# Matrix LSTM layer: head norm on ScalarE behind the next inner products, output gate and skip multiplied out where the gates are made

## The chip, the cores and the metric

The kernel runs on one core of a Trainium2 chip, in one launch. The metric is the device time of an execution in microseconds (us); several executions are timed and the median is given. One further execution is recorded by the hardware profiler, and all rows of a profile come from that one. Engines are named as in the profile: PE is TensorE (matrix products), PEld its loading of weights, DVE VectorE, ACT ScalarE, POOL GpSimd, SP SyncE, which here only issues transfers (DMA).

## The reference

A decoder trunk of two layers, 1024 tokens, width 1024, float32. Each layer has a mixer, a cross-attention into 256 memory tokens and a squared-ReLU MLP; each of these is `h = h + RMSNorm_post(f(RMSNorm_pre(h)))`. The change is in the mixer of the second layer, a matrix LSTM with 4 heads of 256:

```python
def _odd_mixer(hn, w_in, conv_w, conv_b, w_q, w_k, w_v, w_gates, b_gates, g_hnorm, skip, w_out):
    x_m, z = jnp.split(hn @ w_in, 2, axis=-1)
    x_c = jax.nn.silu(_causal_conv(x_m, conv_w, conv_b))
    q, k = per-head products of x_c with w_q, w_k;  v = per-head product of x_m with w_v
    gates = jnp.concatenate([q, k, v], axis=-1).reshape(B, S, 3 * MIX_WIDTH) @ w_gates + b_gates
    h = _mlstm_cell(q, k, v, i_pre, f_pre)
    h = _layernorm(h, g_hnorm.reshape(H, DH)).reshape(B, S, MIX_WIDTH)
    out = (h + skip * x_c) * jax.nn.silu(z)
    return out @ w_out
```

(The lines on q, k and v are shortened.) `_mlstm_cell` runs over chunks of tokens. In each it forms the decayed inner products of queries and keys (`w_intra`), `num = w_intra @ v + w_inter * (q @ C)`, a denominator, `h = num / max(|den|, exp(-m))`, and then carries the state `C` of 256 x 256 a head to the next chunk. `_layernorm` takes the mean and variance of a token over the 256 features of a head.

## The kernel before, in words

Every float32 matrix product that needs its precision is done as three products of rounded parts: a tile is split into a high part (ACT copies it, rounded, line 137) and a low part (DVE or POOL subtracts the two, line 143), and `acc3` (lines 149 to 151) issues high x high, high x low and low x high. So ACT and DVE, and POOL for some weights, have a piece of work for each tile that PE is to use.

SBUF is shared out as 34 units of about 4 KB a partition (`self.u`), 12 weight tiles (`self.wt`) and 3 raw tiles. Weights come through `Stream`: a load on SP's queue into a raw tile, then a split; `Stream.next()` keeps a fixed number of tiles ahead. All engines work in order on lists that the tile scheduler makes from the program text: it runs a model of the engines and takes the ready instruction that stands first in the text, so instructions move ahead of others where their inputs are ready, and the text's order is a priority and not the order itself.

`mix1` has these parts:

- **Projections and gates.** For each head, `front` makes x_m and x_c (convolution, SiLU), feature-major, half of the tokens (512) at a time; `ready` splits them and stores x_c to DRAM (`xd`); `back` makes the gate pre-activations, q and v and stores them. Between `ready` and `back` stands one half of `gate(j)`: 24 products for 128 features of z, SiLU by ACT and DVE (lines 396 to 400), and a store of silu(z) into `zd`. `gate(0)` to `gate(3)` are done in the four heads' turns, `gate(4)` to `gate(7)` behind them, between the first loads of the chunk sweep.
- **Chunk sweep**, 8 chunks of 128 tokens, 8 PSUM banks. `load(c)` brings q, k, v and the decay row; `decay(c)` makes the exponentials; `within(c)` makes the inner products S of queries and keys, multiplies them with the decay (line 1665) and splits them, and makes the weighted keys; `across(c)` multiplies with v and the carried state into `nm` (ACT copies the state's part from PSUM, line 1730, DVE adds the other from PSUM, line 1734), updates C (line 1743) and splits it. The head norm stands at the end of `across`: statistics (lines 1751 to 1758), the power -1/2 on POOL (`rstd`, lines 187 and 188), and four `tensor_scalar` on DVE, one a head (line 1762). `turn(c)` transposes `nm` on PE and multiplies it with the norm's gain out of PSUM (line 1775). `self.side(1, ...)` puts in a piece of independent work for the cross-attention (kt, vt, wk, vo; its weights' low parts are made on POOL, line 143, in pairs of 128x1024).
- **End and output projection.** `skips(c)` loads x_c and silu(z) of a chunk (xg, zg), and POOL makes skip * x_c * silu(z) in two products (lines 1704 and 1705). `gated(c)` multiplies hT with zg, adds xg (DVE, lines 1711 and 1712) and splits the sum into m. `out_proj` multiplies with w_out1 (lines 372 to 375), two PSUM tiles of two banks; `tail` makes the post-norm, adds the residual on POOL (line 306) and prepares the next sub-layer.

The sweep's order in the text:

```python
for c in range(NT):
    across(c)
    if c < NT - 2:
        load(c + 2)
    self.side(1, SIDE_LSTM[c])
    if c < NT - 1:
        within(c + 1)
    if c < NT - 2:
        decay(c + 2)
    if c:
        turn(c - 1)
    ...
```

Of the kernel before, what the change touches and what calls it, by code (L numbers as in the profile page):

```python
# [7 lines left out]
F32 = mybir.dt.float32  # L8
# [3 lines left out]
AF = mybir.ActivationFunctionType  # L12
ALU = mybir.AluOpType
AX = mybir.AxisListType

P = 128
D = 1024
S = 1024
NT = S // P
HALF = 512  # L20
# [57 lines left out]
class Trunk:  # L78
# [81 lines left out]
    def stream_of(self, sub):  # L160

        T, l = self.T, int(sub[-1])
        if sub[:2] == "xa":
            return Stream(self, [self.kv[l][0][j // 4, j % 4].rearrange("p a b -> p (a b)") for j in range(8)], 1, "dve", (6, 7))
        if sub[:3] == "ffn":
            first = [(g, p) for ps in (SEVEN[:2], SEVEN[2:]) for g in (0, 1) for p in ps]
            return Stream(self, first + [(g, p) for g in range(2, GROUPS) for p in SEVEN], 3, make=self.up_weights(l))
        if l == 0:
            return Stream(self, [T["w_in0"][j] for j in (4, 5, 6, 7, 0, 1, 2, 3)] + [T["w_gvr"][j] for j in range(8)], 2)
        return Stream(self, [T["w_in1"][j] for j in (0, 1, 2, 3, 8, 4, 5, 9, 6, 7, 10, 11, 12, 13, 14, 15)], 1)  # L170

    def prefetch(self, n, lo_eng=None):

# [1270 lines left out]
    def mix1(self):  # L1444
        nc, T = self.nc, self.T
        mm = nc.tensor.matmul
        cw, cb = self.const("conv_w"), self.const("conv_b")
        gh, skip = self.const("g_hnorm"), self.const("skip")
        bgt = self.const("b_gates")
        tmask = self.const("tmask")  # L1450
        W = self.take("mix1")

        qd, xd, zd = (self.dram(n, [NT, P, 8, P]) for n in ("qd", "xd", "zd"))
        vd = self.dram("vd", [NT, P, 4, 256])

        def put(dst, half, head, t):
# [5 lines left out]
        with self.psum(6, 1):  # L1462
            gacc = self.u([100, S], F32, "gacc")
            heads, gates = {}, {}
# [83 lines left out]

            def gate(j, halves=(0, 1)):

                if not halves[0]:
                    gates[j] = W.next(), self.u([P, 2, HALF], F32, "sz")
                w, sz = gates[j]
                for half in halves:
                    self.silu(sz[:, half, :], self.feature_major(w, half, "z"), self.t2())
                    nc.sync.dma_start(zd[4 * half:4 * half + 4, :, j, :].rearrange("c p t -> p c t"), sz[:, half, :].rearrange("p (c t) -> p c t", t=P))
                if half:
                    del gates[j]

# [5 lines left out]
            for head in range(4):  # L1565
                if 0 < head < 3:
                    front(head + 1, 0)
                    front(head + 1, 1)
                ops = ready(head, 0)
                gate(head, (0,))  # L1570
                back(head, 0, ops, ws)
                ops = ready(head, 1)
                gate(head, (1,))
                if head < 3:
                    nxt = weights(head + 1)
                back(head, 1, ops, ws)
                ws = nxt
                del heads[head]
# [8 lines left out]
            ig, lf, m, b, tmp = row  # L1587
# [16 lines left out]
            x, y = lf, ig  # L1604
# [75 lines left out]
                            nc.vector.scalar_tensor_tensor(kw[1][:, h, :], k, cl[:, 2, h:h + 1], kw[0][:, h, :].bitcast(F32), ALU.mult, ALU.subtract)  # L1680
                ch[c] = (qp, va, cl, wp, kw)

            gate(4)
            self.side(1, 1)
            load(0)
            gate(5)
            decay(0)
            self.side(1, 1)
            gate(6)
            within(0)  # L1690
            gate(7)
        self.hn = [None, None]
# [1 line left out]
        hT = {}  # L1694
        ms = {}

        sk = {}

        def skips(c):

            xg, zg = self.u([P, 8, P], F32, "xg"), self.u([P, 8, P], F32, "zg")
            for t, src in ((xg, xd), (zg, zd)):
                nc.sync.dma_start(t.rearrange("p a b -> p (a b)"), src[c].rearrange("p a b -> p (a b)"))
            nc.gpsimd.tensor_tensor(xg, xg, skip.unsqueeze(2).broadcast_to([P, 8, P]), ALU.mult)
            nc.gpsimd.tensor_tensor(xg, xg, zg, ALU.mult)
            sk[c] = xg, zg

        def gated(c):

            h, (xg, zg) = hT.pop(c), sk.pop(c)  # L1710
            nc.vector.tensor_tensor(h, h, zg, ALU.mult)
            nc.vector.tensor_tensor(h, h, xg, ALU.add)
            ms[c] = self.parts([P, 8, P], "m")
            self.split(*ms[c], h)

        with self.psum(*PS_LSTM):
# [3 lines left out]
            hbs, wo = {}, []  # L1720

            def across(c):

                qp, va, cl, wp, kw = ch.pop(c)
                nm = self.u([P, 4, 258], F32, "nm")
                for h in range(4):
                    ps = self.p1("num")
# [9 lines left out]
                if c < NT - 1:  # L1737
                    for h in range(4):
                        for e in range(2):
                            ps = self.p1("C")  # L1740
                            self.acc3(ps[:, 0:258], [(tuple(x[:, h, e * P:e * P + P] for x in kw), tuple(x[:, h, :] for x in va))])
                            if c:
                                nc.vector.scalar_tensor_tensor(C[h][:, e, :], C[h][:, e, :], be[:, c, h:h + 1], ps[:, 0:258], ALU.mult, ALU.add)
                            else:
                                nc.vector.tensor_copy(C[h][:, e, :], ps[:, 0:258])
                        self.split(Cp[h][:, 0], Cp[h][:, 1], C[h])
                st = self.sm([P, 4, 4], name="stm1")
                bn = self.sm([P, 4, 6], name="bn")

# [8 lines left out]
                nc.vector.tensor_tensor(s, s, w, ALU.mult)  # L1758
                self.rstd(s, s)
                nc.vector.tensor_tensor(s, s, w, ALU.mult)  # L1760
                for h in range(4):
                    nc.vector.tensor_scalar(nm[:, h, 0:256], nm[:, h, 0:256], st[:, h, 0:1], st[:, h, 3:4], ALU.subtract, ALU.mult)
                hbs[c] = nm

            def turn(c):

                nm = hbs.pop(c)
                hT[c] = self.u([P, 8, P], F32, "hT")
                for g in range(2):
                    ps = self.p1("hT").rearrange("p (a b) -> p a b", b=P)  # L1770
                    for a in range(4):
                        k = 4 * g + a
                        nc.tensor.transpose(ps[:, a, :], nm[:, k // 2, k % 2 * P:k % 2 * P + P], self.ident)
                    w = slice(4 * g, 4 * g + 4)
                    nc.vector.tensor_tensor(hT[c][:, w, :], ps, gh[:, w].unsqueeze(2).broadcast_to([P, 4, P]), ALU.mult)

            load(1)
            decay(1)
# [6 lines that stand above are left out]
                    within(c + 1)  # L1785
                if c < NT - 2:
                    decay(c + 2)
                if c:
                    turn(c - 1)
                if c >= NT - 2:  # L1790
                    skips(c - NT + 2)
                if c == NT - 1:
                    gated(0)
                if c == NT - 2:
                    wo += [self.fetch(T["w_out1"][k], "dve", self.u) for k in (0, 1)]
# [145 lines left out]
```

## Time and profile before

| | |
|---|---|
| median of 3 runs | 2979.53 us (2977.46 to 2980.94) |
| the profiled execution | 2979.67 us; span from first to last instruction 2977.9 us |
| mean granted TensorE clock | 0.980 |
| busy over the span | PE 96%, DVE 64%, ACT 47%, POOL 30% |
| projections and gates | about 1557 to 1812 us |
| chunk sweep | about 1812 to 1997 us |
| its end and the output projection | about 1997 to 2112 us |
| transfers | 385.09 MB, mean 129 GB/s |

A row of the timeline gives start, length, engine, line, operation, output and inputs, and in brackets the time that the engine stood still before it and what ended that. A row by tile or line gives the shortest, median and longest duration in ns. A row of waits gives the total in us, how often, and the longest. In the table of stretches each engine's busy time is followed by its number of instructions; the clock is 1.00 at full speed. Since PE is the busiest engine, the idle time of another engine costs nothing by itself.

### The profile page before, as it was taken

How to read it: one execution, taken by the hardware profiler on the slowest of the kernel's cores; microseconds unless marked ns; L12 is line 12 of the kernel's file. 1: busy time of each engine (PE TensorE's matmuls, PEld its weight loads, DVE VectorE, ACT ScalarE, POOL GpSimd, SP SyncE). 2: the span in 40 equal slices, each digit the busy share in tenths (PEclk: the TensorE clock that was granted, in tenths of full speed). 3: DMA queues.
4: the chain of work that ended last, by engine and by line, in shares of the span. 5: the costliest groups of instructions: out<-in, count | busy, mean ns of one | idle time of the engine just before them, and what ended most of it. 6: DMA issues, size and time to landing. Idle time of an engine off the chain costs nothing. (4 is left out here: it accounts for less than half of the span.)

```text
span 2977.9 us, 37928 instructions
## 1 busy us (share of the span) xinstructions
PE 2846.6 (96%) x14470; PEld 2355.4 (79%) x14470; DVE 1909.4 (64%) x2348; ACT 1402.7 (47%) x2391; POOL 898.2 (30%) x674
## 2 busy tenths in 40 slices
PE   7998999999999999999999999889999999999998
PEld 6777888888887888787867888887788788878776
DVE  4237788754347443799876657887733744458995
ACT  4346666633346455433445565543433655544332
POOL 2204545233330000167050113357533100006723
PEclk9998999999999999999999999999999999999999
DMA  4264544352322333531163345547323233263204
GB/s 160 97 165 147 168 141 148 116 197 71 109 104 90 109 113 136 203 114 64 52 223 96 122 144 178 189 163 251 113 63 121 85 108 112 103 231 111 98 17 142
DMA packets 165222, 385.09 MB, mean 129 GB/s; under 512 B 16748, under 2 KB 66316, under 8 KB 165040
## 3 DMA queue, kind: packets, MB, share of 16 engines
q1 hardware_dynamic: 146608, 349.10, 35.0%
q10 hardware_dynamic: 18432, 33.56, 2.9%
q8 instruction: 114, 1.87, 0.3%
q14 instruction: 68, 0.56, 0.1%
HBM read 267.86 MB, written 113.69 MB: 128 GB/s over the span
## 5 line engine op out<-in xcount | busy, mean ns | idle before, releaser
L143 DVE TENSOR_TENSOR wl<-blk,wh 128x1024 fp32r<-128x1024 f32 x276 | 451.7, 1659 | 320.0 <-ACT wh L137 320.0
L493 POOL TENSOR_TENSOR blk<-blk 128x1024 f32<-128x1024 f32 x80 | 252.4, 3183 | 869.0 <-DVE wl L143 863.5
L137 ACT ACTIVATE wh<-blk 128x1024 fp32r<-128x1024 f32 x276 | 281.8, 1054 | 327.6 <-PE op L561 188.7
L560 PE MATMUL up<-hnh,wh 128*128 128x512 f32 x896 | 356.0, 398 | 9.6 <-ACT hnh L137 5.0
L561 PE MATMUL up<-hnl,wh 128*128 128x512 f32 x896 | 354.5, 396 | 4.8 <-DVE hnl L143 4.8
L562 PE MATMUL up<-hnh,wl 128*128 128x512 f32 x896 | 353.4, 395 | 0.0
L561 PE MATMUL op<-wl,wh 128*128 128x512 f32 x784 | 307.9, 393 | 9.7 <-DVE wl L143 9.6
L560 PE MATMUL op<-wh 128*128 128x512 f32 x784 | 306.3, 395 | 6.2 <-ACT wh L137 6.2
L562 PE MATMUL op<-wh,wl 128*128 128x512 f32 x784 | 306.0, 390 | 0.0
L137 ACT ACTIVATE wh<-raw 128x1024 fp32r<-128x1024 f32 (+1 forms) x163 | 170.6, 1058 | 138.1 <-DMA raw<-hd 25.9
L143 POOL TENSOR_TENSOR wl<-raw,wh 128x1024 fp32r<-128x1024 f32 x66 | 158.9, 2420 | 223.6 <-ACT wh L137 208.3
L560 PEld LDWEIGHTS up<-hnh,wh 128*128 128x128 f32 x896 | 169.1, 189 | 51.3 <-ACT hnh L137 11.4
L561 PEld LDWEIGHTS up<-hnl,wh 128*128 128x128 f32 x896 | 169.3, 189 | 45.5 <-DVE hnl L143 6.3
L562 PEld LDWEIGHTS up<-hnh,wl 128*128 128x128 f32 x896 | 169.3, 189 | 40.1
L143 DVE TENSOR_TENSOR wl<-raw,wh 128x1024 fp32r<-128x1024 f32 (+1 forms) x97 | 126.6, 1315 | 99.7 <-ACT wh L137 99.3
L561 PEld LDWEIGHTS op<-wl,wh 128*128 128x128 f32 x784 | 148.0, 189 | 47.1 <-DVE wl L143 16.4
L560 PEld LDWEIGHTS op<-wh 128*128 128x128 f32 x784 | 149.1, 191 | 39.0 <-ACT wh L137 8.2
L562 PEld LDWEIGHTS op<-wh,wl 128*128 128x128 f32 x784 | 147.8, 188 | 30.5
L187 POOL TENSOR_SCALAR st<-st 128x1 f32<-128x1 f32 x99 | 41.6, 421 | 361.6 <-ACT hn L303 307.4
L306 POOL TENSOR_TENSOR h<-h,hn 128x1024 f32<-128x1024 f32 x47 | 128.4, 2732 | 33.5 <-DVE hn L305 26.2
L673 DVE TENSOR_TENSOR acc<-acc,op 128x512 f32<-128x512 f32 x192 | 123.8, 676 | 4.3 <-PE op L562 4.1
L287 DVE SCALAR_TENSOR_TENSOR hn<-h,st,gain 128x1024 f32<-128x1024 f32 x48 | 101.8, 2122 | 26.1 <-POOL st L188 24.8
(440 smaller groups left out, 6993.5 us busy)
## 6 DMA issues: line engine op xcount, KB each, us to landing
blk<-in_ffn_w_dram SPq DMA_DIRECT2D x120, 512.0 KB, 4.3
h<-h SPq DMA_DIRECT2D x80, 512.0 KB, 4.1
hd<-t ACTq DMA_DIRECT2D x128, 256.0 KB, 2.9
blk<-hd SPq DMA_DIRECT2D x56, 512.0 KB, 4.2
raw<-in_w_in_dram SPq DMA_DIRECT2D x24, 512.0 KB, 4.1
h<-in_x_dram SPq DMA_DIRECT2D x16, 512.0 KB, 6.3
raw<-in_xa_w_k_dram SPq DMA_DIRECT2D x16, 512.0 KB, 3.7
raw<-in_xa_w_v_dram SPq DMA_DIRECT2D x16, 512.0 KB, 3.8
```

The costliest lines, as they stand in the source:

```text
L137: nc.scalar.activation(hi, src, AF.Copy)
L143: e.tensor_tensor(lo, src, hi.bitcast(F32), ALU.subtract)
L187: self.nc.gpsimd.tensor_scalar(dst, src, EPS, None, ALU.add)
L287: nc.vector.scalar_tensor_tensor(hn, h, st[:, 1:2], gpre, ALU.mult, ALU.mult)
L306: nc.gpsimd.tensor_tensor(h, h, t, ALU.add)
L493: eng.tensor_tensor(out, a, b, op)
L560: mm(ps, lh, rh, start=start and not i, stop=False, skip_group_check=True)
L561: mm(ps, lh, rl, start=False, stop=False, skip_group_check=True)
L562: mm(ps, ll, rh, start=False, stop=i == n - 1, skip_group_check=True)
L673: nc.vector.tensor_tensor(dst, dst, ps[i], ALU.add)
```

## The change

The head norm leaves `across` and becomes `norm(c)`, called after `decay(c + 2)` and ahead of `turn(c - 1)`. Its last step, (x - mean) * s, is done on ACT as Identity with scale s and bias -mean * s; DVE makes the bias in one new 128x4 product. `gate(j)` now makes two products for each half: silu(z) times the norm's gain (ACT, stored to `zd`), and skip * x_c * silu(z) (DVE, stored to a new `bd`); both stores are issued by ACT instead of one by SP. In the heads' turns `gate` takes j = 0, 2, 4, 6, whose x_c lies in SBUF, and behind them j = 1, 3, 5, 7, whose x_c is loaded back from `xd`; the weight stream is reordered to match. `norm(c)` loads the chunk's `zd` into the tile hT, and `turn` multiplies the transposed tile with it instead of with the gain. `skips(c)` loads one tile, `bd`, and POOL's two products are gone; `gated(c)` only adds.

```diff
@@ -167,7 +167,7 @@
             return Stream(self, first + [(g, p) for g in range(2, GROUPS) for p in SEVEN], 3, make=self.up_weights(l))
         if l == 0:
             return Stream(self, [T["w_in0"][j] for j in (4, 5, 6, 7, 0, 1, 2, 3)] + [T["w_gvr"][j] for j in range(8)], 2)
-        return Stream(self, [T["w_in1"][j] for j in (0, 1, 2, 3, 8, 4, 5, 9, 6, 7, 10, 11, 12, 13, 14, 15)], 1)
+        return Stream(self, [T["w_in1"][j] for j in (0, 1, 2, 3, 8, 4, 5, 10, 6, 7, 12, 14, 9, 11, 13, 15)], 1)
 
     def prefetch(self, n, lo_eng=None):
 
@@ -1450,7 +1450,8 @@
         tmask = self.const("tmask")
         W = self.take("mix1")
 
-        qd, xd, zd = (self.dram(n, [NT, P, 8, P]) for n in ("qd", "xd", "zd"))
+
+        qd, xd, zd, bd = (self.dram(n, [NT, P, 8, P]) for n in ("qd", "xd", "zd", "bd"))
         vd = self.dram("vd", [NT, P, 4, 256])
 
         def put(dst, half, head, t):
@@ -1548,12 +1549,24 @@
 
             def gate(j, halves=(0, 1)):
 
+                def cols(dst, half):
+                    return dst[4 * half:4 * half + 4, :, j, :].rearrange("c p t -> p c t")
+
                 if not halves[0]:
-                    gates[j] = W.next(), self.u([P, 2, HALF], F32, "sz")
-                w, sz = gates[j]
+                    gates[j] = W.next(), self.u([P, 2, HALF], F32, "sz"), self.u([P, 2, HALF], F32, "bz")
+                w, sz, bz = gates[j]
                 for half in halves:
-                    self.silu(sz[:, half, :], self.feature_major(w, half, "z"), self.t2())
-                    nc.sync.dma_start(zd[4 * half:4 * half + 4, :, j, :].rearrange("c p t -> p c t"), sz[:, half, :].rearrange("p (c t) -> p c t", t=P))
+                    if j % 2:
+                        xc = bz[:, half, :]
+                        nc.sync.dma_start(xc.rearrange("p (c t) -> p c t", t=P), cols(xd, half))
+                    else:
+                        xc = heads[j // 2][2][half][:, 0, :]
+                    z, x = sz[:, half, :], bz[:, half, :]
+                    self.silu(z, self.feature_major(w, half, "z"), self.t2())
+                    nc.vector.scalar_tensor_tensor(x, z, skip[:, j:j + 1], xc, ALU.mult, ALU.mult)
+                    nc.scalar.activation(z, z, AF.Copy, scale=gh[:, j:j + 1])
+                    for dst, t in ((zd, z), (bd, x)):
+                        nc.scalar.dma_start(cols(dst, half), t.rearrange("p (c t) -> p c t", t=P))
                 if half:
                     del gates[j]
 
@@ -1567,10 +1580,10 @@
                     front(head + 1, 0)
                     front(head + 1, 1)
                 ops = ready(head, 0)
-                gate(head, (0,))
+                gate(2 * head, (0,))
                 back(head, 0, ops, ws)
                 ops = ready(head, 1)
-                gate(head, (1,))
+                gate(2 * head, (1,))
                 if head < 3:
                     nxt = weights(head + 1)
                 back(head, 1, ops, ws)
@@ -1680,13 +1693,13 @@
                             nc.vector.scalar_tensor_tensor(kw[1][:, h, :], k, cl[:, 2, h:h + 1], kw[0][:, h, :].bitcast(F32), ALU.mult, ALU.subtract)
                 ch[c] = (qp, va, cl, wp, kw)
 
-            gate(4)
+            gate(1)
             self.side(1, 1)
             load(0)
-            gate(5)
+            gate(3)
             decay(0)
             self.side(1, 1)
-            gate(6)
+            gate(5)
             within(0)
             gate(7)
         self.hn = [None, None]
@@ -1698,18 +1711,13 @@
 
         def skips(c):
 
-            xg, zg = self.u([P, 8, P], F32, "xg"), self.u([P, 8, P], F32, "zg")
-            for t, src in ((xg, xd), (zg, zd)):
-                nc.sync.dma_start(t.rearrange("p a b -> p (a b)"), src[c].rearrange("p a b -> p (a b)"))
-            nc.gpsimd.tensor_tensor(xg, xg, skip.unsqueeze(2).broadcast_to([P, 8, P]), ALU.mult)
-            nc.gpsimd.tensor_tensor(xg, xg, zg, ALU.mult)
-            sk[c] = xg, zg
+            sk[c] = self.u([P, 8, P], F32, "bg")
+            nc.sync.dma_start(sk[c].rearrange("p a b -> p (a b)"), bd[c].rearrange("p a b -> p (a b)"))
 
         def gated(c):
 
-            h, (xg, zg) = hT.pop(c), sk.pop(c)
-            nc.vector.tensor_tensor(h, h, zg, ALU.mult)
-            nc.vector.tensor_tensor(h, h, xg, ALU.add)
+            h = hT.pop(c)
+            nc.vector.tensor_tensor(h, h, sk.pop(c), ALU.add)
             ms[c] = self.parts([P, 8, P], "m")
             self.split(*ms[c], h)
 
@@ -1744,6 +1752,11 @@
                             else:
                                 nc.vector.tensor_copy(C[h][:, e, :], ps[:, 0:258])
                         self.split(Cp[h][:, 0], Cp[h][:, 1], C[h])
+                hbs[c] = nm, cl
+
+            def norm(c):
+
+                nm, cl = hbs[c]
                 st = self.sm([P, 4, 4], name="stm1")
                 bn = self.sm([P, 4, 6], name="bn")
 
@@ -1758,21 +1771,24 @@
                 nc.vector.tensor_tensor(s, s, w, ALU.mult)
                 self.rstd(s, s)
                 nc.vector.tensor_tensor(s, s, w, ALU.mult)
+
+                nc.vector.scalar_tensor_tensor(w, st[:, :, 0], -1.0, s, ALU.mult, ALU.mult)
                 for h in range(4):
-                    nc.vector.tensor_scalar(nm[:, h, 0:256], nm[:, h, 0:256], st[:, h, 0:1], st[:, h, 3:4], ALU.subtract, ALU.mult)
+                    nc.scalar.activation(nm[:, h, 0:256], nm[:, h, 0:256], AF.Identity, bias=st[:, h, 2:3], scale=st[:, h, 3:4])
+                hT[c] = self.u([P, 8, P], F32, "hT")
+                nc.sync.dma_start(hT[c].rearrange("p a b -> p (a b)"), zd[c].rearrange("p a b -> p (a b)"))
                 hbs[c] = nm
 
             def turn(c):
 
                 nm = hbs.pop(c)
-                hT[c] = self.u([P, 8, P], F32, "hT")
                 for g in range(2):
                     ps = self.p1("hT").rearrange("p (a b) -> p a b", b=P)
                     for a in range(4):
                         k = 4 * g + a
                         nc.tensor.transpose(ps[:, a, :], nm[:, k // 2, k % 2 * P:k % 2 * P + P], self.ident)
                     w = slice(4 * g, 4 * g + 4)
-                    nc.vector.tensor_tensor(hT[c][:, w, :], ps, gh[:, w].unsqueeze(2).broadcast_to([P, 4, P]), ALU.mult)
+                    nc.vector.tensor_tensor(hT[c][:, w, :], ps, hT[c][:, w, :], ALU.mult)
 
             load(1)
             decay(1)
@@ -1785,6 +1801,7 @@
                     within(c + 1)
                 if c < NT - 2:
                     decay(c + 2)
+                norm(c)
                 if c:
                     turn(c - 1)
                 if c >= NT - 2:
```

## The prediction

> **What bounds the kernel now.** I read the page first (engines' shares), then busy time by stretch over the odd mixer, then PE's waits there, then the timelines of DVE, POOL and PE around one gap. The page says that TensorE (PE) is nearly always busy, so only time in which PE stands still or runs at a lower granted clock can be won.
>
> ```profile
> PE 2846.6 (96%) x14470; PEld 2355.4 (79%) x14470; DVE 1909.4 (64%) x2348; ACT 1402.7 (47%) x2391; POOL 898.2 (30%) x674
> ```
>
> The stretches are: projections and gates (front), the step over to the chunk sweep, the sweep, its end with the loading of w_out1, and the output projection. Columns: length, busy time of PE, PEld, DVE, ACT, POOL, granted clock, DMA.
>
> ```profile
> 1557.00:1812.00 255.00, 249.59 (x1212) 203.84 (x1211) 153.37 (x214) 141.17 (x243) 36.41 (x30) 1.00 0.42 130
> 1812.00:1840.00 28.00, 22.70 (x172) 21.79 (x172) 25.27 (x49) 15.74 (x29) 8.72 (x6) 0.94 0.58 188
> 1840.00:1997.00 157.00, 142.35 (x1059) 137.58 (x1060) 136.40 (x291) 88.93 (x152) 68.31 (x40) 0.95 0.52 176
> 1997.00:2036.00 39.00, 31.13 (x144) 25.20 (x144) 29.11 (x38) 15.14 (x20) 25.92 (x11) 0.87 0.71 252
> 2036.00:2112.00 76.00, 70.05 (x317) 55.84 (x316) 64.36 (x43) 25.01 (x45) 63.30 (x39) 1.00 0.50 178
> ```
>
> PE loses 157 - 142.35 = 14.7 us of standing in the sweep and 0.05 x 157 = 7.9 by its clock; at the sweep's end 7.9 and 0.13 x 39 = 5.1; in the projection 6.0 and nothing. That makes 22.5 + 13.0 + 6.0 = 41.5 us, all there is to win. The front stands only 5.4 us. Who ends PE's waits (total us, times, longest), first in the sweep, then behind it:
>
> ```profile
> PE C L149 <- DVE nm L1734: 14.4, 5, 3.1
> PE num L149 <- DVE vt L143: 2.3, 1, 2.3
> ```
> ```profile
> PE op L375 <- DVE ml L143: 4.6, 4, 2.2
> PE vo L149 <- DVE nm L1734: 4.5, 1, 4.5
> PE op L373 <- DVE wl L143: 3.2, 1, 3.2
> PE tp L219 <- DVE hn L287: 1.3, 1, 1.3
> ```
>
> So five gaps of 2.9 us wait for DVE's add that empties PSUM (L1734). What holds DVE there, with POOL and PE beside it:
>
> ```profile
> 1862.81 5.05 DVE L1762 TENSOR_SCALAR nm<-nm,stm 128x256 f32<-128x256 f32 x4
> 1867.78 0.41 DVE L1734 TENSOR_TENSOR nm<-nm,num 128x258 f32<-128x258 f32 x1
> ```
> ```profile
> 1862.27 2.41 POOL L143 TENSOR_TENSOR wl<-raw,wh 128x1024 fp32r<-128x1024 f32 x1 [2.36 <-PE num L151]
> ...
> 1864.68 2.38 POOL L143 TENSOR_TENSOR wl<-raw,wh 128x1024 fp32r<-128x1024 f32 x1
> ```
> ```profile
> 1868.25 0.58 PE L149 MATMUL C<-vah,kwh 128*128 128x258 f32 x1 [3.13 <-DVE nm L1734]
> ```
>
> Four normalising instructions (L1762), directly ahead of the adds, take 5.05 us while POOL runs two subtractions of 2.4 us. All of L1762 (shortest, median, longest in ns), and then its busy time on DVE in the sweep:
>
> ```profile
> L1762 DVE TENSOR_SCALAR nm<-nm,stm x32: 397/408/2503, 1826.7 to 2014.0; 128x256 f32<-128x256 f32 x32
> ```
> ```profile
> 1840.00:1997.00 157.00, 31.50 (x24) 0.95 0.52 176
> ```
>
> Undisturbed, one takes 0.397 us, so four would take 1.6; the longest waits out a whole POOL operation, and the median 0.408 hides it. In the sweep that comes to 31.5 us for six chunks, 5.25 us each. These, not the adds, make the gap. The Trainium skill (SBUF — State Buffer, "Who interferes with whom") states that a DVE instruction in a 2-port mode, or with two SBUF inputs, and a GpSimd instruction that reads SBUF block each other for a whole instruction, and that ACT never waits so. By that rule the move is worth the blocked time too, and the 5.05 beside 2.41 and 2.38 agrees.
>
> **The change, step by step.**
>
> *Sweep: L1762 to ACT, and the norm moved.* DVE loses 5.25 us a chunk where a gap is 2.9, so 2.35 us are to spare. Against this stand the statistics, which the new order puts behind `within` and `decay`. They exist now, spread between the C updates:
>
> ```profile
> L1755 DVE BATCH_NORM_STATS2 bn<-nm 128x6 f32<-128x256 f32 x32 | 13.0, 415 | 0.1
> L1665 DVE TENSOR_TENSOR ew<-ew,S 128x512 f32<-128x512 f32 x7 | 4.8, 684 | 16.0 <-PE S L1664 16.0
> L1756 DVE BATCH_NORM_AGGREGATE stm<-bn 128x2 f32<-128x6 f32 x32 | 5.2, 168 | 0.0
> L1752 DVE TENSOR_TENSOR stm<-stm,cl 128x4 f32<-128x4 f32 x8 | 2.2, 273 | 0.0
> L1757 DVE TENSOR_TENSOR stm<-stm 128x4 f32<-128x4 f32 x8 | 1.3, 160 | 0.1
> ```
>
> For a chunk that is 4 x (0.415 + 0.168) = 2.3 us and seven small ones (one of them the new product) near 0.16: about 3.5 us. If they lie in DVE's wait for S (16.0 / 7 = 2.3 us a chunk), the gap goes; if all lie ahead of the adds, 3.5 - 2.35 = 1.1 us of each gap stays. The clock loss follows the gaps. I take 70% of 22.5: **-16**, ends 0 and -22.5. Next would be PE itself: DVE keeps (136.4 - 31.5) of 157.
>
> On ACT come four Identity instructions a chunk, SBUF to SBUF, which the trace lacks. Nearest rows: the same width without a scale tile, and with one:
>
> ```profile
> L1736 ACT ACTIVATE nm<-num x4: 364/380/394, 1815.3 to 1816.1; 128x258 f32<-128x258 f32 x4
> L1730 ACT ACTIVATE nm<-num,cl x28: 457/482/532, 1834.1 to 1997.2; 128x258 f32<-128x258 f32 x28
> ```
>
> I take 0.48, the row with a tile as scale, ends 0.36 and 0.53: 1.9 us a chunk in an engine busy 88.9 of 157; hidden. What is queued behind them on ACT is the draining of num (L1730); PE would wait for that if they came late. The Trainium skill (ScalarE: Activation LUTs, "What ACT_TABLE_LOAD costs") gives 186 ns, 0.833 ns an element and 93 ns a pointer operand; an estimate from that page is 0.585 us with two pointers, 2.3 us a chunk, and the sum would be the same.
>
> SP gets one 512 KB load for hT a chunk in the sweep, which leaves the projection (zg there). DMA is busy 0.52 in the sweep, and hT is read a whole chunk later: 0, ends 0 and +3 (one 3.1 us gap, if a weight came late). The turned tile is multiplied by zd instead of a broadcast gain in the same instruction: 0.
>
> *Sweep's end: -8.* Now gated(0) stands between DVE's adds, and waits for POOL's second product:
>
> ```profile
> 1996.89 1.99 DVE L1711 TENSOR_TENSOR hT<-hT,zg 128x1024 f32<-128x1024 f32 x1
> 1998.80 0.41 DVE L1734 TENSOR_TENSOR nm<-nm,num 128x258 f32<-128x258 f32 x1
> ...
> 2001.14 3.35 DVE L1712 TENSOR_TENSOR hT<-hT,xg 128x1024 f32<-128x1024 f32 x1 [0.85 <-POOL xg L1705]
> 2004.42 0.41 DVE L1734 TENSOR_TENSOR nm<-nm,num 128x258 f32<-128x258 f32 x1
> ```
> ```profile
> L1711 DVE TENSOR_TENSOR hT<-hT,zg x8: 1212/2366/3417, 1996.9 to 2101.8; 128x1024 f32<-128x1024 f32 x8
> ```
>
> One product and the wait go (1.99 + 0.85 = 2.8 us), and the add may shrink from 3.35 to the 1.2 of its kind undisturbed (1212 ns). The 4.5 us gap keeps 0 to 1.6. The 3.2 us wait for wl stands behind a like wait for POOL, but partly behind weight loads, which stay. 60% of 13.0 is 8; ends -3 (the 2.8 alone) and -13.
>
> *Projection: -5.* POOL loses both products, DVE one, and what is left on DVE runs undisturbed:
>
> ```profile
> L1704 POOL TENSOR_TENSOR xg<-xg,c_skip x8: 2660/2884/4678, 1993.1 to 2097.3; 128x1024 f32<-128x1024 f32 x8
> L1705 POOL TENSOR_TENSOR xg<-xg,zg x8: 3222/3255/3270, 1997.9 to 2100.3; 128x1024 f32<-128x1024 f32 x8
> L143 DVE TENSOR_TENSOR ml<-hT,mh x8: 1211/2065/3421, 2014.3 to 2111.1; 128x1024 fp32r<-128x1024 f32 x8
> ```
>
> A chunk costs POOL 2.88 + 3.26 = 6.1 us less, DVE 2.4 less for the product gone and 0.9 less (2.07 to 1.21) for ml. The waits for ml and hn (4.6 + 1.3) should go; the add of h on POOL (L306) remains. Ends 0 and -6.
>
> *Front: +2.* Sixteen half gates each gain a product on DVE, a scaled copy on ACT and two stores issued by ACT instead of one by SP; eight halves gain a 256 KB load on SP. Nearest rows:
>
> ```profile
> L1500 DVE SCALAR_TENSOR_TENSOR xc<-xm,c_conv_w,xc x48: 736/749/1807, 1568.5 to 1714.8; 128x512 f32<-128x512 f32 x24, 128x511 f32<-128x511 f32 x8, 128x510 f32<-128x510 f32 x8, 128x509 f32<-128x509 f32 x8
> L1492 ACT ACTIVATE xm<-xm x16: 577/597/602, 1564.6 to 1707.8; 128x512 f32<-128x512 f32 x16
> ```
> ```profile
> L575 ACTq DMA_DIRECT2D hd<-t x128: 326/326/379, 894.0 to 2646.9; - x128
> ```
>
> DVE 16 x 0.749 = 12 us on 153 of 255; ACT 16 x (0.597 + 2 x 0.326) = 20 us on 141. Both fit under PE's 249.6, which is the cover: uncovered, ACT's 20 us would show. Ends 0 and +20; I take +2, near the covered end, since ACT keeps 94 us free. The reordered weight stream loads the same tiles: 0.
>
> *Step over: +1.* The last gate's extra copy and issues (1.25 us) can come ahead of ACT's first drains (L1736): ends 0 and +2.
>
> Sum: -16 - 8 - 5 + 2 + 1 = -26. The profiled execution took 2979.67 us (span 2977.9), the median is 2979.53, so 2953.7, told as **2954**. Full recovery of all three gives 2979.7 - 41.5, or 2938.
>
> **Rivals.**
>
> *The stall finds another victim.* POOL keeps its subtractions. L1752, a 128x4 operation with two SBUF inputs, averages 0.273 us where its neighbour L1757 takes 0.16, so some of these are already held up. If statistics meet a POOL pair (4.8 us), DVE reaches the adds as late as now; or ACT's Identity waits for POOL's power (L188) behind such a pair, and num is drained as late. Either leaves the sweep where it is: -8 - 5 + 3 = -10, so 2970. For: the pair recurs in each chunk. Against: DVE has idle time to place them in, and a gap takes a blocked operation just ahead of the adds. The rule of the Trainium skill told above (SBUF — State Buffer, "Who interferes with whom") allows for this case too, since it counts two-input instructions of any size.
>
> *Slower: ACT in the front.* ACT works in order. Its copy waits for DVE's two products, its stores for the copy; behind them stand the drains of xm and q that PE needs. Gains of 29 us over 16 halves are used up at 1.8 us of PE time each; a hold of 3 us each costs 48 and ends at 2979.7 - 29 + 48 = 2999. For: PE has no slack there. Against: ACT and DVE stand idle over a third of it.
>
> *No change.* The gaps were filled by order alone and PE's next instruction waits for something as late (a weight, a slot of the 34 units, one more of which hT and bz hold): within 6 us of 2980.
>
> **How the numbers follow.** Forecast (2938 to 2964) 0.62; other victim (2965 to 2974) 0.20; no change 0.10; slower 0.08. A difference within 0.2%, 6 us, is about what a measurement of this kernel can't tell from no change. Faster by more 0.82, within 0.10, slower 0.08. The range 2938 to 2974 takes in the first two cases and leaves out the others; the likeliest alone is 2938 to 2964.
>
> **What would show it.** Right: no DVE work on nm between hT's products and the adds in the sweep, PE's waits for nm near zero, the clock there at 0.98 or more; POOL under half busy in the projection, ml near 1.2 us. Wrong: gaps of 2 to 3 us remain under another releaser (ACT's L1730 or DVE's statistics), or PE stands in the front for ACT. The forecast fails most likely by DVE's new order: the instructions may be placed differently from what the program text suggests.

## The result, and the profile after

The changed kernel takes 2955.32 us (median, 2954.62 to 2957.31) beside 2980.24 us for the kernel before on the same chip: a ratio of 0.9918, with a 95% interval of 0.9901 to 0.9935. That is about 25 us, or 0.8%. The profiled execution took 2957.31 us, its span 2955.4 us, at a mean granted clock of 0.984 (0.980 before).

The same stretches as before, in the same columns (front, step over, sweep, end, projection):

```profile
1555.00:1816.00 261.00, 251.27 (x1202) 205.47 (x1201) 164.38 (x229) 149.29 (x255) 36.51 (x29) 0.99 0.48 148
1816.00:1836.00 20.00, 16.00 (x131) 15.38 (x130) 16.52 (x37) 11.35 (x19) 5.07 (x5) 1.00 0.50 160
1836.00:1986.00 150.00, 146.04 (x1111) 138.85 (x1110) 131.34 (x284) 108.56 (x191) 67.16 (x42) 0.99 0.66 224
1986.00:2020.00 34.00, 28.38 (x150) 23.72 (x149) 22.96 (x33) 18.57 (x25) 9.28 (x5) 0.95 0.83 302
2020.00:2101.00 81.00, 80.60 (x369) 65.37 (x368) 54.32 (x49) 30.47 (x56) 34.60 (x33) 1.00 0.41 141
```

In the sweep PE now stands 150 - 146.04 = 4.0 us instead of 14.7, and its clock costs 0.01 x 150 = 1.5 us instead of 7.9. In the projection it stands 0.4 us instead of 6.0. In the front it stands 261 - 251.27 = 9.7 us instead of 5.4, and the clock there has dropped from 1.00 to 0.99.

Stretches cut by hand compare badly between kernels, since work slides across the cuts. So the kernels are set side by side by landmarks on PE: the first product of x_m, the first product of num with v, the first of num with C, the last of num, and the first and last product of out_proj. Each is taken at the start of the product. For the sweep these rows give them, before (first two) and after, as the first start of the one and the last start of the other:

```profile
L149 PE MATMUL num<-Cp,qh x56: 276/284/389, 1830.8 to 1996.0; 128*128 128x258 f32 x56
L149 PE MATMUL num<-vah,ewp x32: 276/282/386, 1809.2 to 1996.3; 128*128 128x258 f32 x32
```
```profile
L149 PE MATMUL num<-Cp,qh x56: 279/286/419, 1836.2 to 1985.9; 128*128 128x258 f32 x56
L149 PE MATMUL num<-vah,ewp x32: 277/282/581, 1815.5 to 1986.2; 128*128 128x258 f32 x32
```

In us between landmarks:

| kernel | front | step | sweep | end | projection |
|---|---|---|---|---|---|
| before | 252.4 | 21.6 | 165.5 | 20.3 | 106.9 |
| changed | 260.3 | 20.7 | 150.0 | 19.7 | 95.5 |
| difference | +7.9 | -0.9 | -15.5 | -0.6 | -11.4 |

Up to x_m the two differ by 1.6 us (1556.8 and 1555.2), behind the projection by 0.4. The sum of the five is -20.5, the spans differ by 22.5. Up to x_m all kernels of this document do the same work, and its first product starts between 1549.9 and 1556.8 us in their profiled executions, so a few us of a single execution's time are not the change's.

What ends PE's waits in the sweep after the change:

```profile
PE num L149 <- ACT ewp L137: 1.9, 1, 1.9
PE C L149 <- DVE C L1751: 1.1, 5, 0.2
PE C L149 <- DVE nm L1742: 0.7, 2, 0.4
PE num L149 <- DVE kwl L1693: 0.2, 1, 0.2
```

The row that had 14.4 us in five gaps (now line 1742) has 0.7. The same place of a chunk, DVE's timeline and then POOL's:

```profile
1914.79 0.68 DVE L1791 TENSOR_TENSOR hT<-hT 128x512 f32<-128x512 f32 x1
1915.38 1.88 DVE L1775 SCALAR_TENSOR_TENSOR stm<-stm 128x4 f32<-128x4 f32 x1
1917.18 0.41 DVE L1742 TENSOR_TENSOR nm<-nm,num 128x258 f32<-128x258 f32 x1
```
```profile
1914.84 2.40 POOL L143 TENSOR_TENSOR wl<-raw,wh 128x1024 fp32r<-128x1024 f32 x1 [2.37 <-PE num L151]
1917.18 0.10 POOL L1649 MEMSET v<- 128x8 f32 x1
1917.25 2.38 POOL L143 TENSOR_TENSOR wl<-raw,wh 128x1024 fp32r<-128x1024 f32 x1
```

POOL's pair is still there, and DVE still waits out an operation of it ahead of the addition. But it is one wait of 1.88 us on a 128x4 product (line 1775), where four normalising instructions took 5.05. DVE was not freed of POOL; its blocking moved onto the small operations. The DVE groups of them that are held up, in the sweep and its end (busy us, mean ns), with one split beside them that took about as long before (1218 ns on the mean):

```profile
L1775 DVE SCALAR_TENSOR_TENSOR stm<-stm 128x4 f32<-128x4 f32 x8 | 11.1, 1393 | 0.1
L143 DVE TENSOR_TENSOR ewp<-ew,ewp 128x512 fp32r<-128x512 f32 x7 | 8.9, 1274 | 2.3 <-ACT ewp L137 2.1
L1773 DVE TENSOR_TENSOR stm<-stm 128x4 f32<-128x4 f32 x8 | 5.6, 702 | 1.9 <-POOL stm L188 1.9
L1771 DVE TENSOR_TENSOR stm<-stm 128x4 f32<-128x4 f32 x8 | 5.6, 696 | 0.2
L1770 DVE TENSOR_TENSOR stm<-stm 128x4 f32<-128x4 f32 x8 | 5.0, 626 | 0.1
L1765 DVE TENSOR_TENSOR stm<-stm,cl 128x4 f32<-128x4 f32 x8 | 3.0, 369 | 0.0
```

Undisturbed, such a 128x4 operation takes 0.16 us (line 1757 of before). The five small groups therefore hold 11.1 + 5.6 + 5.6 + 5.0 + 3.0 - 40 x 0.16 = 24 us of blocked time. All five read two tensors; the 128x4 RECIPROCAL and TENSOR_REDUCE of the same norm, which read one, stayed at 0.17 and 0.15 us. Before, the 32 normalising instructions held this:

```profile
L1762 DVE TENSOR_SCALAR nm<-nm,stm 128x256 f32<-128x256 f32 x32 | 40.3, 1319 | 0.1
```

Of the 32 x 1.319, all but 32 x 0.397 is blocked time: 29.5 us. So most of the blocked time stayed (24 of 29.5 us); what changed is where it falls, and in what pieces.

Of the 7.9 us lost in the front, 5 stand in one place, PE's timeline and then ACT's:

```profile
1786.88 0.33 PE L1662 MATMUL Rt<-c_ident,R 128*128 128x128 f32 x1 [4.99 <-ACT R L1627]
```
```profile
1775.17 0.42 ACTq L1569 DMA_DIRECT2D bd<-bz  x1
1775.86 0.38 ACTq L1569 DMA_DIRECT2D zd<-sz  x1
...
1784.69 1.06 ACT L137 ACTIVATE vah<-v 128x1032 fp32r<-128x1032 f32 x1 [5.27 <-DMA v<-vd]
...
1785.77 1.05 ACT L1627 ACTIVATE R<-row 4x1024 f32<-4x1024 f32 x1
```

PE waits to transpose chunk 0's decay row R. ACT, which makes its exponential (line 1627), stands for 5.27 us at the split of v (vah), which comes first in its list and waits for a load. That load was issued by SP at 1775.53, between two stores that ACT issues, and ACT starts on v 9.2 us later. In the kernel before, R came ahead of vah, and vah followed its load by 5.6 us (1775.06 to 1780.70):

```profile
1777.99 1.06 ACT L1614 ACTIVATE R<-row 4x1024 f32<-4x1024 f32 x1
1780.70 1.07 ACT L137 ACTIVATE vah<-v 128x1032 fp32r<-128x1032 f32 x1 [0.98 <-DMA v<-vd]
```

The gap is paid twice. In the stretch around it, before (first row) and after (second), PE's busy time falls by 4.9 us, and its clock, by 0.11, costs about 0.11 x 15 = 1.6:

```profile
1780.00:1795.00 15.00, 14.95 (x74) 12.19 (x73) 9.12 (x15) 11.16 (x18) 4.77 (x2) 1.00 0.37 111
```
```profile
1780.00:1795.00 15.00, 10.01 (x46) 8.45 (x45) 8.42 (x15) 10.26 (x18) 0.00 (x0) 0.89 0.52 153
```

That makes 6.5 of the 7.9 us; for the rest no single row accounts.

### The profile page after: what moved, and what is told of

The parts are those of the page before. It is cut to its first block, busy times and chain, and to the rows that moved or that the text cites. A ratio compares the mean times of both kernels' runs of the same rounds, so it can differ in the third digit from the quotient of the medians.

```text
span 2955.4 us, 37974 instructions
## 1 busy us (share of the span) xinstructions
PE 2840.4 (96%) x14470; PEld 2349.9 (80%) x14470; DVE 1880.0 (64%) x2332; ACT 1428.0 (48%) x2439; POOL 841.4 (28%) x658
## 5 line engine op out<-in xcount | busy, mean ns | idle before, releaser
L560 PEld LDWEIGHTS up<-hnh,wh 128*128 128x128 f32 x896 | 169.2, 189 | 51.5 <-ACT hnh L137 11.4
L306 POOL TENSOR_TENSOR h<-h,hn 128x1024 f32<-128x1024 f32 x47 | 131.3, 2794 | 32.0 <-DVE hn L305 24.9
L305 DVE SCALAR_TENSOR_TENSOR hn<-op,st,gain 128x1024 f32<-128x1024 f32 x32 | 41.1, 1284 | 118.6 <-POOL st L188 118.6
```

What stands on the lines that cost most here:

```text
L306: nc.gpsimd.tensor_tensor(h, h, t, ALU.add)
L560: mm(ps, lh, rh, start=start and not i, stop=False, skip_group_check=True)
```

## Experiments: the two halves of the change

Theory: the sweep's gain is the four normalising instructions leaving DVE, which POOL blocks; the end's and the projection's gain is POOL's skip products. Rivals: the norm's new place does it, or POOL's pair finds something else on DVE.

**The last step back on DVE, in the norm's new place.**

```diff
-                nc.vector.scalar_tensor_tensor(w, st[:, :, 0], -1.0, s, ALU.mult, ALU.mult)
                 for h in range(4):
-                    nc.scalar.activation(nm[:, h, 0:256], nm[:, h, 0:256], AF.Identity, bias=st[:, h, 2:3], scale=st[:, h, 3:4])
+                    nc.vector.tensor_scalar(nm[:, h, 0:256], nm[:, h, 0:256], st[:, h, 0:1], st[:, h, 3:4], ALU.subtract, ALU.mult)
```

> The changed kernel, but the norm's last step is again four tensor_scalar on DVE (and the bias product is gone); place of the norm, gates and skip stay as changed. Theory: PE's gaps in the sweep came from blocked DVE work directly ahead of the adds that empty PSUM, so with four instructions back there the gaps of 2 to 3 us and the slow clock return, some 10 to 14 us: 2965 to 2969, PE waiting for nm by DVE at least 8 us in total in the sweep. Rival: the new place of the norm alone made the gain: within 3 us of the changed kernel's 2955, waits for nm under 3 us.

It took 2973.84 us, a ratio of 0.9983 (0.9974 to 0.9993) to before. The sweep is 166.0 us between landmarks, so all of its gain is gone, and the gaps are back (PE's waits behind the front):

```profile
PE C L149 <- DVE nm L1742: 11.4, 5, 3.1
```

The loss is larger than expected. The new place by itself, with the work left on DVE, wins nothing in the sweep.

**Only the last step moved: the kernel before, with the Identity on ACT inside `across`.**

> The kernel before, with one edit: the norm's last step is four Identity on ACT, with the bias product on DVE, left at the end of across; gates and skip as before. Theory: most of the sweep's gain is this edit: 10 to 15 us faster than before, 2965 to 2970, PE's wait for nm by DVE in the sweep under 4 us. Rival: without the norm's new place the gaps stay: within 4 us of before.

It took 2959.13 us, a ratio of 0.9937 (0.9922 to 0.9952): 20 us won, more than expected, 18.6 of them in the sweep. It is 146.9 us, shorter than the changed kernel's 150.0; PE's waits for the addition (line 1734) in it are down to this row:

```profile
PE C L149 <- DVE nm L1734: 0.5, 2, 0.2
```

Front (252.0) and projection (107.1) are those of before. With the run above, this shows that the engine does it, and not the place.

**Only the gates' half: the changed kernel, with the norm on DVE and back in `across`.**

> The gates' half of the change alone: silu(z) times gain and skip * x_c * silu(z) made in the gates, stores by ACT, zd loaded into hT; the norm stays at the end of across and on DVE as before. Theory: the end and projection win 11 to 13 us, the front loses 6 to 8, the sweep stays as before with gaps of 2.5 to 3 us: 2973 to 2977. Rival (the tail's gain needs the sweep's): end and projection within 4 us of before, 2982 to 2988.

It took 2975.89 us, a ratio of 0.9989 (0.9980 to 0.9999). The front is 259.3 us (+6.9), end and projection together 114.8 (-12.4), as in the changed kernel. But the sweep is 170.1, 4.6 longer than before, with new waits of 10.3 us for a low part of vt made on DVE beside the old ones for nm. The projection's gain and the front's loss belong to this half, and alone it is worth next to nothing.

**POOL's two skip products given to DVE, in the kernel before.**

```diff
-            nc.gpsimd.tensor_tensor(xg, xg, skip.unsqueeze(2).broadcast_to([P, 8, P]), ALU.mult)
-            nc.gpsimd.tensor_tensor(xg, xg, zg, ALU.mult)
+            nc.vector.tensor_tensor(xg, xg, skip.unsqueeze(2).broadcast_to([P, 8, P]), ALU.mult)
+            nc.vector.tensor_tensor(xg, xg, zg, ALU.mult)
```

> The kernel before, with POOL's two skip products a chunk moved to DVE, so that DVE has 2.4 us more work a chunk of its own and POOL 6.1 us less. Theory (in the end and projection DVE lost its time by being blocked, and by waiting for POOL): faster than before by 5 to 10 us, 2970 to 2975, with ml and the add near 1.2 us wherever POOL isn't adding h. Rival (it was the amount of DVE work): slower by 2 to 10 us, DVE's busy time in the projection above before's 64 of 76 us and PE's waits for ml up from 4.6.

It took 2969.71 us, a ratio of 0.9972 (0.9962 to 0.9983), just below the 2970 to 2975 that were expected; the projection falls from 106.9 to 98.0 us, although DVE has more to do. The subtraction that makes ml, on DVE:

```profile
L143 DVE TENSOR_TENSOR ml<-hT,mh x8: 1212/1224/3423, 2008.1 to 2091.8; 128x1024 fp32r<-128x1024 f32 x8
```

Its median falls from 2.07 to 1.22 us. What held up the projection was POOL's work beside DVE's, not the amount of DVE's. Two ways are mixed in that. POOL's products block DVE's operations, and DVE's addition (line 1712) waited for the second of them, 10.1 us in six waits, none of which is left here. This run does not part them.

**POOL's pairs taken away: the low parts of the cross-attention's weights on DVE, in the kernel before.**

```diff
-                W = Stream(self, blocks, 1, "pool")
+                W = Stream(self, blocks, 1, "dve" if l else "pool")
```

> The kernel before, with the low parts of the second layer's cross-attention weights made by DVE (1.2 us each) instead of POOL (2.4 us) in the sweep. Theory (POOL's subtractions block L1762): L1762's mean falls from 1.3 us to 0.4 in the sweep, some 26 us of DVE time, about what the 23 or more subtractions then cost DVE; the gaps before the adds shrink to under 1.5 us or move. Time 2966 to 2982. Rival (L1762 is slow for another reason, such as its own stride or the semaphores between its four): its mean stays over 1 us.

It took 2958.37 us, a ratio of 0.9935 (0.9921 to 0.9950): faster than expected, and as much as the move to ACT. All 32 normalising instructions, still on DVE, now run as if alone:

```profile
L1762 DVE TENSOR_SCALAR nm<-nm,stm x32: 399/405/413, 1822.2 to 1997.9; 128x256 f32<-128x256 f32 x32
```

The sweep is 143.9 us, the shortest but one of all runs, but part of that is only moved: the step before it is 26.1 us instead of 21.6, with more of PE's products in it, and the end is 27.4 instead of 20.3. The three together are 197.4 us, against 207.4 before and 189.1 with the Identity on ACT. Another 6.7 us are won in the projection (100.2 us), and no run tells why. At the end PE has one new wait:

```profile
PE hT L1773 <- DVE nm L1762: 12.0, 1, 12.0
```

This shows the mechanism from the other side: the same instructions on the same engine cost a third (0.405 against 1.319 us) once POOL's subtractions are gone. The Trainium skill (SBUF — State Buffer, "Who interferes with whom") names this blocking; the trace agrees for 128x256 (0.405 and 1.319 us), and the 128x4 products of line 1775 show it for operands of four elements too.

## Experiments: the loss in the front, and what is left

**Chunk 0's v split by POOL, so that ACT does not stand at it.**

```diff
-                self.split(*va, v)
+                self.split(*va, v, *(() if c else ("pool", "pool")))
```

> The changed kernel, with chunk 0's v split into its two parts by POOL alone instead of ACT and DVE, nothing else. Theory: the front's loss is mostly one wait, in which ACT stood on the late load of v ahead of the exponential into R that PE needed; with v off ACT, the 5 us wait for Rt and the slow clock behind it go: 5 to 7 us faster than the changed kernel, 2948 to 2950. Rival: the front's loss is the added work and store issues on ACT, spread over it: within 2 us of 2955, other gaps in the place of this one.

It took 2951.17 us, a ratio of 0.9910 (0.9893 to 0.9926); the front is 256.9 us, a little less won than expected. The wait for R is gone, but not all of the loss: v is late here too (issued at 1770.88, first read at 1780.20, 9.3 us), ACT is held again, in front of a zd store, and PE waits 2.1 us for what stands behind it:

```profile
1780.54 0.18 ACT L1664 ACTIVATE cl<-Rt 128x16 f32<-128x16 f32 x1 [2.24 <-DMA v<-vd]
```

But PE has the same wait, 2.1 us, in the run with gate 1's stores on SP, further down, where v is not late, so it can't be put down to v alone.

**The gates' stores issued by SP again.**

```diff
-                        nc.scalar.dma_start(cols(dst, half), t.rearrange("p (c t) -> p c t", t=P))
+                        nc.sync.dma_start(cols(dst, half), t.rearrange("p (c t) -> p c t", t=P))
```

> The changed kernel, with the gates' two stores a half issued by SP instead of ACT. Theory (the front's loss is the order at one place): no change beyond 3 us either way, since ACT was not what PE waited for elsewhere; the Rt wait moves only if v's load lands at another time. Rival (the 32 issues on ACT cost the front): 4 to 8 us faster than the changed kernel, 2947 to 2951.

It took 2949.62 us, a ratio of 0.9904 (0.9891 to 0.9917). My theory of no change missed; the rival's size held. The front is 254.6 us, and PE waits there no more for ACT's R. ACT's rows:

```profile
1777.36 1.06 ACT L1627 ACTIVATE R<-row 4x1024 f32<-4x1024 f32 x1
1778.52 1.07 ACT L137 ACTIVATE vah<-v 128x1032 fp32r<-128x1032 f32 x1
```

R is ahead of vah again, and v, issued at 1773.36, is there at most 5.2 us later. PE's stretch of 15 us at this place is full, at a clock of 1.00:

```profile
1778.00:1793.00 15.00, 15.00 (x74) 12.36 (x73) 9.91 (x17) 11.44 (x19) 2.23 (x1) 1.00 0.59 168
```

**Only gate 1's four stores on SP**, the two around v's load among them.

> The changed kernel with the stores of gate 1 alone on SP (4 of the 32), the others on ACT. Theory: what costs the front its 5 us is only what ACT issues just ahead of chunk 0's v, so the front falls from 260 to 254-256, PE's 5.0 us wait for the exponential R is gone, and the kernel takes 2949 to 2952, as with all stores on SP. Rival: the 28 other stores, spread over the heads' turns and the later gates, cost as much: front 257 to 260, kernel 2952 to 2956.

It took 2952.79 us, a ratio of 0.9915 (0.9902 to 0.9928), at the edge between the two expectations; the front decides. It is 255.5 us, so four stores of 32 bring back 4.8 of the 5.7 us that all of them bring. R (1775.43) stands ahead of vah, and the load lands in 5.9 us:

```profile
1778.30 1.06 ACT L137 ACTIVATE vah<-v 128x1032 fp32r<-128x1032 f32 x1 [1.81 <-DMA v<-vd]
```

The stores still stand 0.4 us ahead of the load and 0.6 us behind it, but on the load's own queue. So most of the loss hangs on what ACT itself issues around that load. The other versions agree. With ACT's stores around the load and v's split on ACT (the changed kernel, the norm back on DVE, the gates' half) the front is 260.3, 257.3 and 259.3 us; with SP's stores there (this run, the one before it and two further down) it is 253.8 to 255.5. So one front alone is good to about 3 us. Two things change together in these runs, the order of ACT's list and the landing (9.2 against 5.9 us). Only v's split on POOL parts them. In that run, the first of this section, and in the next one, which has it too (front 254.7 us), R comes early although v is late (9.3 and 8.7 us), and 3.4 and 5.6 us come back. That points to the order as the larger part.

**The 128x4 products on POOL**, on top of the v split there, so that they cannot be blocked on DVE:

```diff
...
-                nc.vector.tensor_tensor(s, s, w, ALU.mult)
-                nc.vector.scalar_tensor_tensor(w, st[:, :, 0], -1.0, s, ALU.mult, ALU.mult)
+                nc.gpsimd.tensor_tensor(s, s, w, ALU.mult)
+                nc.gpsimd.tensor_tensor(w, st[:, :, 0], s, ALU.mult)
```

(The sign of the mean goes into one more 128x4 product on DVE, ahead of the power.)

> The changed kernel with chunk 0's v split by POOL, and the norm's two small products behind the power (128x4) on POOL too, so that DVE has none of them ahead of the adds; DVE negates the mean instead. Theory: beyond the 5 to 7 us of the first edit, the blocked small products (1.4 us and 0.7 us on average, 17 us in eight chunks) go, of which PE sees 1 to 4 us: 2945 to 2949. Rival: POOL's queue makes ACT's Identity later (its operations wait behind a pair of 4.8 us), num is drained late: 2950 to 2965.

It took 2952.89 us, a ratio of 0.9921 (0.9907 to 0.9935): no gain over the split of v alone. The rival's time held, and PE does wait for ACT's drains of num (line 1738):

```profile
PE C L149 <- ACT nm L1738: 3.7, 8, 0.8
```

But the Identity is not late, as the rival had it. ACT waits for POOL's product once, 2.1 us in the first chunk. In five later chunks the products are there in time, and all four Identity stand ahead of the drains in ACT's list, where in the changed kernel two drains come first. Here, then in the changed kernel:

```profile
1911.18 2.11 ACT L1777 ACTIVATE nm<-nm,stm 128x256 f32<-128x256 f32 x4
1913.15 0.51 ACT L1738 ACTIVATE nm<-num,cl 128x258 f32<-128x258 f32 x1
```
```profile
1915.63 0.50 ACT L1738 ACTIVATE nm<-num,cl 128x258 f32<-128x258 f32 x1
...
1916.94 0.51 ACT L1738 ACTIVATE nm<-num,cl 128x258 f32<-128x258 f32 x1
1917.30 2.10 ACT L1777 ACTIVATE nm<-nm,stm 128x256 f32<-128x256 f32 x4
```

**Stores on SP and the norm back in `across`, on ACT.**

> The changed kernel with the gates' stores on SP, and the norm back in `across` (its last step still on ACT). Theory: the norm's place behind within and decay is worth little (putting the last step alone on ACT gave a sweep of 146.9 us against 150.0 with the new place too), so the sweep is 144 to 150 and the kernel 2944 to 2952, within 3 us of the version with the stores on SP alone (2949.6). Rival: the new place matters, since the statistics again stand between the additions out of PSUM: gaps for DVE's addition return, the sweep is 153 to 160 and the kernel 2956 to 2964.

It took 2950.23 us, a ratio of 0.9908 (0.9895 to 0.9921). The time is the theory's, the sweep is not: 152.2 us between its landmarks, with 24.9 before it and 16.1 behind. Step, sweep and end together are 193.2 us, against 189.7 with the new place and the stores on SP. So the place is worth about 3.5 us there, but with the norm in `across` the projection is 2.4 us shorter (93.3 against 95.7), and the runs' times do not tell the whole from nothing (0.6 us between the medians).

**Stores on SP, and POOL's pairs on DVE.**

> The changed kernel with the gates' stores on SP, and the low parts of the cross-attention's weights of layer 1 (line 143, 128x1024) made by DVE instead of POOL. Theory: with POOL's long subtractions gone from the sweep nothing blocks DVE there, and the 128x4 operations fall from 0.6-1.4 us back to 0.16; but PE stands only 4 us of 150 in the sweep now, so at most 4 are won, and DVE takes on 37 subtractions of 1.24 us: 2944 to 2952. Rival: the sweep's end grows as in the earlier trial on the kernel before (27.4 us against 20.3), when DVE has both the additions and the subtractions to do: 2953 to 2962.

It took 2954.82 us, a ratio of 0.9923 (0.9907 to 0.9939); the rival held. The bias products run undisturbed:

```profile
L1775 DVE SCALAR_TENSOR_TENSOR stm<-stm x8: 156/161/170, 1830.8 to 2003.5; 128x4 f32<-128x4 f32 x8
```

So the 1.39 us of the changed kernel came from POOL. The sweep is 143.5 us, but the step before it is 28.0 and the end 26.4, with a wait of 9.7 us for the last Identity.

Of these versions the one with the stores on SP has the lowest median, 5.7 us below the changed kernel's, though on another chip, where the kernel before is 1.9 us faster too. The intervals of the two ratios overlap (0.9891 to 0.9917, and 0.9901 to 0.9935), so that it is faster rests on the profiles, where a wait of 5.0 us and its clock loss are gone and the front is shorter in all four versions with SP's stores, and not on the times alone.

## Why the prediction was right, and where not

The prediction was 2954 us, measured are 2955.32. Its terms, beside what the landmarks show:

| step | said | measured |
|---|---|---|
| sweep | -16 | -15.5 |
| sweep's end and projection | -8 - 5 | -12.0 |
| front | +2 | +7.9 |
| step over | +1 | -0.9 |

*Sweep.* The size and the cause held: gaps ahead of the addition out of PSUM, made by blocked normalising instructions. One step was wrong within it. I let DVE lose 5.25 us a chunk, 31.5 us in the sweep; its busy time in the sweep went from 136.40 of 157 to 131.34 of 150, 5 us in all. The rival "the stall finds another victim" named the thing that happened: the 128x4 operations are held up instead. Its price (nothing won in the sweep) did not come, because a blocked operation there costs 0.4 to 1.4 us on the mean, only one of them stands directly ahead of the additions, and PE rides out an addition 1.9 us late: 5.05 - 1.88 = 3.2 us (an estimate, from two different chunks) is about the gap of 3.13 us that is gone. PE's longest wait for an addition is 0.4 us. The lost clock came back with the gaps, 0.95 to 0.99.

*Identity.* I took 0.48 us, the row of one with a scale tile; measured are 0.59, above my upper end of 0.53:

```profile
L1777 ACT ACTIVATE nm<-nm,stm x32: 586/592/631, 1837.1 to 2000.5; 128x256 f32<-128x256 f32 x32
```

The estimate of 0.585 from the Trainium skill (ScalarE: Activation LUTs, "What ACT_TABLE_LOAD costs") was the better one, and the trace agrees with it. It changed nothing: 0.4 us a chunk in an engine busy 108.56 of 150. The gate's copy, with a scale tile, was low for the same reason: 0.724 us where I took 0.597 from a row without one.

*End and projection.* The sum held. The landmarks put 0.6 us of it ahead of the first product of out_proj and 11.4 behind; my two stretches were cut elsewhere, so -8 and -5 can't be judged apart. What I gave as a sign, ml near 1.2 us, is wrong:

```profile
L143 DVE TENSOR_TENSOR ml<-hT,mh x8: 1215/3422/3432, 1988.9 to 2082.4; 128x1024 fp32r<-128x1024 f32 x8
```

POOL's addition of h (line 306), which stayed, blocks it for 2.2 us in five of the eight chunks. But no wait for ml is left on PE, and POOL is busy 34.60 of 81 there, under half as told. So ml ends in time even when it is blocked: its own length was not what PE waited for.

*Front.* This is the term that was mis-sized, by 6 us, and one of the signs of being wrong came true: PE stands in the front for ACT. I had ACT's 20 us hidden in its idle time, and all but one wait of 5.0 us were; no other wait for ACT there is longer than 0.6 us. What I missed is that the place and the order of the issues matter. ACT's list got v's split ahead of R's exponential, and the load it waits for came into use 3.5 us later after its issue than before (9.2 against 5.6). The rival "ACT in the front" had ACT's order as its mechanism, but priced it as a hold in every half gate; it came once. The terms come to -20.5 us where I summed -26; another 2.0 went outside of the mixer's stretches (1.6 us ahead of x_m, 0.4 behind the projection), where the change does nothing and executions differ by more than that. The profiled execution, from which the terms are taken, is 22.4 us faster than that of before, and is the slowest of its four; the medians differ by 24.9. So that the median came within 2 us of the forecast is in part luck: the mixer's own terms alone would put it near 2959 us, which the range takes in too.

## What to carry to other kernels

When an engine's instruction is long only because another engine blocks it, look for the place where the delay ends in the bound engine's wait, and clear that place; the blocked time itself may stay and cost nothing elsewhere. The kernel shows two ways that were each worth 20 us alone, to take the blocked work to an engine that isn't blocked, or the blocking work away; done together they were worth no more than one (2954.82 us, beside 2949.62 with the first way alone). And cost a transfer's issue by what stands next to it: of the front's 7.9 us, 4.8 hung on four stores issued by ACT around one awaited load.

## What was unexpected of the hardware

- A 128x4 product on DVE with both inputs in SBUF took up to 2.29 us beside POOL's 128x1024 subtractions, 0.16 without them: a factor of 14 on an instruction that no count of elements would show.

```profile
L1775 DVE SCALAR_TENSOR_TENSOR stm<-stm x8: 168/1658/2286, 1834.7 to 1998.8; 128x4 f32<-128x4 f32 x8
```

- A 512 KB load took 8.1 to 9.3 us to its first use in the five traces where ACT issued two 256 KB stores within 0.4 us of it, and 5.9 us with the same stores on SP's queue around it. Why the queue should matter so much, no run shows.
- One gap of 5.0 us went with a granted clock of 0.89 over 15 us, and in the first experiment 16.3 us of gaps, none longer than 3.1 us, came with 0.94 over 150 us (the columns are those of the stretches):

```profile
1836.00:1986.00 150.00, 133.74 (x975) 127.34 (x975) 138.15 (x288) 85.75 (x150) 60.96 (x36) 0.94 0.61 206
```
